# A gate's lower weight halves by accumulating transfers, and a planner's transfer figures refitted

## The chip, the cores and the metric

The kernel runs on one core of one Trainium2 chip. The metric is the device time of one execution in microseconds, and the median of several executions is what is compared.

## What is computed

The reference is a backbone of two layers over 256 latent and 256 context tokens of width 1024, all in float32. Each layer is a half-step SwiGLU feed-forward block (FFN1), a token mixer, and a second half-step block (FFN2), each with a shift, a scale and a gate that come from a conditioning vector ("adaLN"); the last layer carries the latent tokens alone from the mixer on. Cut to what matters here:

```python
mod = (silu_c @ w_ada[l] + b_ada[l])[:, None, :]
sh1, sc1, g1, sh2, sc2, g2, sh3, sc3, g3 = jnp.split(mod, N_MOD, axis=-1)
x = x + 0.5 * g1 * swiglu(modulate(rmsnorm(x), sh1, sc1), ffn1_w1[l], ffn1_w3[l], ffn1_w2[l])
...
o_lat, o_ctx = token_mixer(...)
x = x + g2 * o_lat
x = x + 0.5 * g3 * swiglu(modulate(rmsnorm(x), sh3, sc3), ffn2_w1[l], ffn2_w3[l], ffn2_w2[l])
```

The mixer has one combined input projection. One part of it is the retention branch's output gate, `ret_g` (1024 columns): the branch's result is `silu(g_raw) * n @ w_ret_out`, where `n` is the normalised retention. The change concerns the weights of this part.

## The kernel before

**Precision by three products.** Every float32 product with weights is made of three matmuls in a reduced 32-bit type: upper half of the weights by upper half of the activations, lower half by upper half, upper half by lower half (`mm3`). The weights come as chunks of 128 x 1024 float32 (512 KB) that SP loads into one of four `raw` buffers. `split_w` (L564) makes the two halves of a chunk: ScalarE (ACT in the profile) casts `raw` into one of four `wh` buffers, and VectorE (DVE) subtracts that from `raw` into one of four `wl` buffers:

```python
hi, lo = plan.new("wh", n, F32R), plan.new("wl", n, F32R)
act.copy(out=hi, in_=raw)
dve.tensor_tensor(out=lo, in0=raw, in1=hi, op=ALU.subtract)
```

**FFN steps.** A step of an FFN block multiplies the normalised tokens by one chunk of the first and one of the third weight matrix. ACT takes one PSUM result `m` through SiLU into `t`; DVE multiplies `t` by the other (`t<-t,m`), ACT or DVE casts the product to its upper half (`CAST t<-t`), and DVE subtracts for the lower half (`t<-t,t`). This is called the product chain below. Later steps multiply both halves by the second weight matrix, and DVE adds the result to the residual (`x<-m,mod,x`).

**adaLN beside it.** The conditioning products are done on DVE, not on PE: each chunk of `w_ada` (512 KB, also through the `raw` buffers) is multiplied by the broadcast vector `crow` and summed along its row by one SCALAR_TENSOR_TENSOR, `junk<-raw,crow`, once or twice for a chunk (latent and context vector). `ada_fill` (L781) puts these between the steps of the FFN blocks and `ada_flush` (L786) puts the rest at their end.

**The mixer's gate stage.** After the other projections, a loop at L1433 goes over eight chunks of the gate's weights. `g_step(i)` (L1117) makes 24 matmuls from a chunk (512 columns in layer 0, 256 in layer 1), a Tanh on ACT and one DVE operation. Around it stand the retention's steps for heads in pairs: state, scores, masks, output with a normalisation (statistics on DVE, a power on GpSimd, here POOL: `s<-s,mhalf`), and splits of queries and keys. POOL also multiplies masks (128x384, 128x128) and subtracts for some lower halves (`64x512` in layer 0, `64x256` in layer 1).

**What sets the order.** Nothing is issued while the program is built: every instruction becomes a `Node` with a cost, and `order()` (L249) runs a list scheduler over all nodes with a model of each engine, of buffers (slots of each kind) and of transfers; the order that it finds for each engine is then emitted (`emit`, L358; all of it has line L368). In the model an SP transfer occupies SP for 475 ns, starts at least 1100 ns after its issue, behind the one before, and runs at 400 bytes a ns. At the program's start, PE is given `N_KEEP` = 5 fills (matmuls on a tile of ones, `a<-ones`, in a range of low priority, L1524) beside 20 first ones.

Of the kernel before, what the change touches and what calls it, by code (L numbers as in the profile page):

```python
# [14 lines left out]
AF = mybir.ActivationFunctionType  # L15
# [27 lines left out]
N_PE_ADA = 5  # L43
N_KEEP = 5
URGENT = 1000
# [114 lines left out]
class Node:  # L160


    __slots__ = ("calls", "engine", "cost", "table", "port", "prio", "index", "waits", "after", "bufs", "new", "ready", "start", "end")

    def __init__(self, engine, prio, index):
        self.engine, self.prio, self.index = engine, prio, index
        self.calls, self.cost, self.table, self.port = [], 0.0, None, False
        self.waits, self.after, self.bufs, self.new = set(), [], {}, []
        self.ready, self.start, self.end = 0.0, None, None


class Plan:
# [8 lines left out]

    COLD = 7000.0

    def __init__(self, tc):
# [64 lines left out]
    def order(self):  # L249
# [16 lines left out]
        stuck = {k: [] for k in self.kinds}  # L266
        dma, table, port = 0.0, None, 0.0
        for n in nodes:
# [19 lines left out]
        while len(done) < len(nodes):  # L288
# [36 lines left out]
            if e == "SP":  # L325
                clock[e] = now + 475.0
                n.end = dma = max(now + 1100.0, dma) + n.cost
            else:
                if n.table not in (None, table):
                    now, table = now + self.TABLE, n.table  # L330
                if n.port:

                    now = max(now, port)
                    port = now + n.cost
                slow = 2.0 if e == "PE" and now < self.COLD else 1.0
                n.end = clock[e] = now + slow * n.cost
# [35 lines left out]
class Engine:  # L372
# [5 lines left out]
    def __getattr__(self, method):  # L378
        call = getattr(self.real, method)

        def record(*args, **kwargs):
            views = [v for v in list(args) + list(kwargs.values()) if isinstance(v, View)]
            out = [v for k in ("out", "accum_out") if isinstance(v := kwargs.get(k), View)]
            if "out" not in kwargs and args and isinstance(args[0], View):
                out.append(args[0])
            reads = [v for v in views if not any(v is o for o in out)]

            table = {AF.Silu: 0, AF.Exp: 1, AF.Tanh: 1}.get(args[2]) if method == "activation" else None
            return self.plan.add(self.name, call, args, kwargs, out, reads, self.cost(method, out, reads, kwargs), table,
                                 self.port(method, out, reads, kwargs))  # L390

        return record

    def port(self, method, out, reads, kwargs):

        if self.name == "POOL":
            return method != "memset"
        if self.name != "DVE" or any(v.buf.kind in ("m", "a") for v in out + reads):
# [4 lines left out]
    def cost(self, method, out, reads, kwargs):  # L403
# [5 lines left out]
        if self.name == "SP":  # L409
            return big.shape[0] * n * 4 / 400.0  # L410
        if self.name == "PE":
# [10 lines left out]
        if self.name == "ACT":  # L422
            return 0.834 * n + (50.0 if psum else 93.0) + 91.0 * pointers + (96.0 if "accum_out" in kwargs else 0.0)
        if self.name == "POOL":
            if kwargs.get("op") == ALU.pow:
                return 300.0 + 165.0 * n
# [10 lines left out]
def kernel(  # L437
# [121 lines left out]
    def step(fn, *chunks):  # L559
        steps.append((chunks, fn))  # L560

    def split_w(raw, n, kind):
# [8 lines left out]
        else:  # L571
            hi, lo = plan.new("wh", n, F32R), plan.new("wl", n, F32R)
            act.copy(out=hi, in_=raw)
            dve.tensor_tensor(out=lo, in0=raw, in1=hi, op=ALU.subtract)
        return Pair(hi, lo)
# [377 lines left out]
    def mixer(l, nrm_in, nrm_out, full):  # L953
# [485 lines left out]
        for i in range(8):  # L1439
            if i % 2 == 0:  # L1440
                step(ret_state(i // 2))
                step(ret_scores(i // 2))
                if i >= 2:
                    step(ret_out(i // 2 - 1))
            step(g_step(i), W("g", i))
            if i % 2 == 0:
# [290 lines left out]
```

## Time and profile before

| | us |
|---|---|
| median of three executions | 2145.7 |
| lowest, highest | 2140.36, 2147.9 |
| the profiled execution, its own time | 2144.34 |
| its span in the profile | 2142.6 |
| PE busy | 2112.4 (99%) |
| DVE busy | 1402.9 (65%) |
| ACT busy | 745.1 (35%) |
| POOL busy | 150.6 (7%) |
| mean granted clock of PE | 0.991 |

All rows come from the one profiled execution. A busy PE is one on which matmuls follow each other; at half the clock the same matmuls take longer and PE is just as busy, so the number of matmuls in a stretch says more than the busy share. The page counts one matmul of the program as one or, where it is not in the reduced type, as two records. The chain that ended last is followed back from the last instruction through whatever released each step. The full page has 40 slices of the span, which are too coarse for stalls of a few microseconds: those are read from the timeline of PE, in which each row ends with the idle time ahead of it.

### The profile page before, as it was taken

The page shows a single profiled execution, that of the slowest core. Times are in us where ns is not written, and L with a number is a line of the kernel's source. Part 1 is how long each engine was busy: PE and PEld are TensorE (multiplying, and loading weights), DVE is VectorE, ACT ScalarE, POOL GpSimd, SP SyncE. Part 2 cuts the span into 40 slices and gives each one's busy share as a digit, 9 for nine tenths or more (in the row PEclk, how much of TensorE's full clock was granted, in tenths as well). Part 3 has the DMA queues.
Part 4 walks back from the last instruction along what each step waited for, and adds up shares of the span by engine and source line. Part 5 has one row for each costly group of instructions (what it writes and reads, how often), then busy time and mean ns, then how long its engine had stood idle before and what let it go on. Part 6 is the DMA issues. An engine that isn't in the chain of part 4 may idle for free.

```text
span 2142.6 us, 29830 instructions
## 1 busy us (share of the span) xinstructions
PE 2112.4 (99%) x11630; PEld 1800.7 (84%) x11630; DVE 1402.9 (65%) x2599; ACT 745.1 (35%) x1225; POOL 150.6 (7%) x172
## 2 busy tenths in 40 slices
PE   9999999999999999999999999999999999999998
PEld 6888788987788888988878898888889879999998
DVE  6898785668679435888755473433337967766665
ACT  4222122476433223422212242221225744344433
POOL 0000000211132000100000010000002112100000
PEclk8999999999999999999999999999999999999999
DMA  8476564221121433466665432333233312474663
GB/s 315 148 219 190 181 189 141 91 84 60 60 70 60 128 112 104 138 199 212 189 187 175 139 119 70 109 97 97 90 98 95 116 60 88 149 264 142 205 187 109
DMA packets 87070, 293.76 MB, mean 137 GB/s; under 512 B 9617, under 2 KB 12817, under 8 KB 86929
## 3 DMA queue, kind: packets, MB, share of 16 engines
q1 hardware_dynamic: 86930, 291.87, 43.6%
q8 instruction: 91, 1.49, 0.3%
q14 instruction: 49, 0.40, 0.1%
HBM read 290.78 MB, written 1.05 MB: 136 GB/s over the span
## 4 chain that ended last, share of the span: by engine, by line
PE 71%; DVE 11%; issue 8%; DMA 7%; POOL 1%; ACT 0%; SPq 0%; POOLq 0%; DVEq 0%; ACTq 0%
PE m L368 66%; DMA raw<-in_w_ada_dram 5%; PE a L368 5%; DVE junk L368 5%; DVE t L368 3%; DVE wl L368 2%; DMA t<-in_w_ada_dram 1%; DVE s L368 1%; DVE u L368 1%; POOL s L368 0%; DMA wh<-in_w_ada_dram 0%; POOL t L368 0%; DVE x L368 0%; ACT t L368 0%; DMA raw<-in_w3a_dram 0%
## 5 line engine op out<-in xcount | busy, mean ns | idle before, releaser
L368 PE MATMUL m<-t,wh 128*128 128x512 f32 (+1 forms) x6248 | 1646.8, 351 | 12.2 <-DVE t L368 11.8
L368 PEld LDWEIGHTS m<-t,wh 128*128 128x128 f32 x6248 | 1092.8, 189 | 180.7 <-DVE t L368 14.9
L368 PE MATMUL m<-t,wl 128*128 128x512 f32 (+1 forms) x3124 | 1086.0, 349 | 0.0
L368 ACT CAST wh<-raw 128x1024 fp32r<-128x1024 f32 (+1 forms) x398 | 409.2, 1029 | 959.3 <-PE m L368 824.6
L368 PEld LDWEIGHTS m<-t,wl 128*128 128x128 f32 x3124 | 589.3, 189 | 82.4
L368 DVE TENSOR_TENSOR wl<-raw,wh 128x1024 fp32r<-128x1024 f32 (+1 forms) x398 | 476.5, 1198 | 259.6 <-ACT wh L368 258.6
L368 DVE SCALAR_TENSOR_TENSOR junk<-raw,crow 128x1024 f32<-128x1024 f32 x220 | 268.8, 1222 | 109.9 <-DMA raw<-in_w_ada_dram 106.6
L368 DVE SCALAR_TENSOR_TENSOR x<-m,mod,x 128x256 f32<-128x256 f32 x192 | 86.3, 479 | 124.4 <-PE m L368 124.1
L368 ACT ACTIVATE t<-m 128x512 f32<-128x512 f32 (+1 forms) x155 | 79.3, 513 | 248.1 <-PE m L368 244.0
L368 DVE TENSOR_TENSOR t<-t,t 128x512 fp32r<-128x512 f32 (+7 forms) x252 | 145.4, 585 | 5.0 <-ACT t L368 2.4
L368 DVE TENSOR_TENSOR t<-t,m 128x512 f32<-128x512 f32 (+1 forms) x91 | 54.3, 597 | 109.2 <-PE m L368 103.7
L368 POOL TENSOR_TENSOR s<-s,mhalf 128x2 f32<-128x2 f32 (+1 forms) x31 | 35.5, 1149 | 1163.4 <-DVE s L368 1163.2
L368 PE MATMUL m<-wh,t 128*128 128x512 f32 x288 | 92.1, 399 | 0.0
L368 PE MATMUL a<-t,t 128*64 128x256 f32 (+3 forms) x512 | 87.2, 351 | 4.8 <-DVE t L368 2.8
L368 PEld LDWEIGHTS a<-t,t 128*128 128x128 f32 (+1 forms) x512 | 66.0, 175 | 22.3 <-ACT t L368 4.9
L368 PE MATMUL m<-t,t 128*128 128x256 f32 (+1 forms) x480 | 76.0, 310 | 0.3 <-DVE t L368 0.3
L368 PEld LDWEIGHTS m<-t,t 128*128 128x128 f32 x480 | 65.2, 191 | 5.5 <-issue 1.2
L368 PEld LDWEIGHTS m<-wh,t 128*128 128x128 f32 x288 | 53.2, 188 | 12.6 <-issue 1.2
L368 ACT CAST t<-t 128x512 fp32r<-128x512 f32 (+4 forms) x112 | 55.9, 526 | 11.5 <-DVE t L368 8.9
L368 PE MATMUL m<-wl,t 128*128 128x512 f32 x144 | 56.9, 395 | 0.0
L368 ACT ACTIVATE t<-u,mod 128x256 fp32r<-128x256 f32 x88 | 39.7, 500 | 28.8 <-DVE u L368 28.8
L368 POOL MEMSET t<- 32x512 f32 x32 | 16.1, 528 | 473.7 <-DVE junk L368 257.3
(105 smaller groups left out, 1045.7 us busy)
## 6 DMA issues: line engine op xcount, KB each, us to landing
raw<-in_w_ada_dram SPq DMA_DIRECT2D x122, 512.0 KB, 4.2
raw<-in_w_m_dram SPq DMA_DIRECT2D x76, 512.0 KB, 3.5
raw<-in_w1b_dram SPq DMA_DIRECT2D x44, 512.0 KB, 3.9
raw<-in_w3b_dram SPq DMA_DIRECT2D x44, 512.0 KB, 3.8
raw<-in_w1a_dram SPq DMA_DIRECT2D x41, 512.0 KB, 3.6
raw<-in_w3a_dram SPq DMA_DIRECT2D x41, 512.0 KB, 3.6
raw<-in_w2a_dram SPq DMA_DIRECT2D x32, 512.0 KB, 3.5
raw<-in_w2b_dram SPq DMA_DIRECT2D x32, 512.0 KB, 3.6
```

Of the source, the lines that this page charges most:

```text
L368: call(*[resolve(v) for v in args], **{k: resolve(v) for k, v in kwargs.items()})
```

## The change

Three things are changed.

1. In both layers the gate's chunks get the kind "d". For these, ACT writes `-raw` into the lower buffer (a second ACT operation on the chunk), rounded as the type of that buffer demands, and a transfer issued by POOL adds `raw` to it: what is left is `raw` less its rounded value. There are 16 such chunks, so 16 DVE subtractions go, 16 ACT operations and 16 transfers inside SBUF come. The chunk's `raw` buffer is now held until the transfer has landed.
2. The planner's figures for transfers are others: the first may start at 2000 ns, an issue takes 560 ns, a transfer starts at least 2000 ns after it and runs at 380 bytes a ns. A transfer on POOL is billed 870 ns of POOL, 2913 ns of the transfers' time and 1800 ns until its end is seen.
3. `N_KEEP` is 20.

```diff
-N_KEEP = 5
+N_KEEP = 20
...
+    FIRST, ISSUE, LATENCY, RATE = 2000.0, 560.0, 2000.0, 380.0
...
-        dma, table, port = 0.0, None, 0.0
+        dma, table, port = self.FIRST, None, 0.0
...
             if e == "SP":
-                clock[e] = now + 475.0
-                n.end = dma = max(now + 1100.0, dma) + n.cost
+                clock[e] = now + self.ISSUE
+                n.end = dma = max(now + self.LATENCY, dma) + n.cost
+            elif n.moved:
+                clock[e] = now + n.cost
+                dma = max(now + self.LATENCY, dma) + n.moved
+                n.end = dma + 1800.0
...
+            if self.name == "POOL" and method == "dma_start":
+                node.moved += 1.5 * out[0].shape[0] * math.prod(out[0].shape[1:]) * 4 / 270.0
...
-            return method != "memset"
+            return method not in ("memset", "dma_start")
...
-            return big.shape[0] * n * 4 / 400.0
+            return big.shape[0] * n * 4 / Plan.RATE
...
+            if method == "dma_start":
+                return 870.0
...
             act.copy(out=hi, in_=raw)
-            dve.tensor_tensor(out=lo, in0=raw, in1=hi, op=ALU.subtract)
+            if kind == "d":
+                act.activation(lo, raw, AF.Copy, scale=-1.0)
+                pool.dma_start(out=lo, in_=raw, accum_op=ALU.add)
+            else:
+                dve.tensor_tensor(out=lo, in0=raw, in1=hi, op=ALU.subtract)
...
-            step(g_step(i), W("g", i))
+            step(g_step(i), W("g", i, "d"))
```

Since the planner's figures enter every decision of `order()`, operations move on DVE, ACT, PE and POOL far from the gate stage too. SP issues the same transfers in the same order, and PE does the same matmuls but for 15 more fills. Of the fills, before the change two stood ahead of the first matmul of the first FFN step and three a little later, each ahead of one accumulation group; now seven stand ahead of the first matmul and thirteen (eleven of them in a row) at the later place. At the start PE also broadcasts `crow` by eight small matmuls: before, three of them stood among the matmuls of the first norms; now all eight stand ahead of these.

**VectorE near the end of FFN1 in layer 0**, before the change. `junk` is an adaLN sum, `t2_1853<-t2_1853,m1_1849` the product of the last FFN step, the CAST and `t11_1921` its two halves, `mod` a finished modulation, `wl` a chunk's lower half:

```order
L368 SCALAR_TENSOR_TENSOR junk_66,s14_1610<-raw0_1797,crow_65 128x1024
L368 TENSOR_TENSOR wl0_1865<-raw1_1770,wh0_1855 128x1024
L368 TENSOR_SCALAR mod0_5_98<-mod0_5_98 128x8
L368 TENSOR_TENSOR mod0_5_98<-s14_1610,sm_64 128x8
L368 TENSOR_SCALAR mod0_5_98<-mod0_5_98 128x8
L368 SCALAR_TENSOR_TENSOR junk_66,s15_1889<-raw0_1867,crow_65 128x1024
L368 TENSOR_TENSOR t2_1853<-t2_1853,m1_1849 128x512
L368 TENSOR_TENSOR wl1_1904<-raw2_1832,wh1_1895 128x1024
L368 CAST t48_1909<-t2_1853 128x512
L368 SCALAR_TENSOR_TENSOR junk_66,s16_1916<-raw0_1867,crow_65 128x1024
L368 TENSOR_TENSOR t11_1921<-t2_1853,t48_1909 128x512
```

The same place after the change:

```order
L375 SCALAR_TENSOR_TENSOR junk_66,s14_1653<-raw3_1818,crow_65 128x1024
L375 TENSOR_TENSOR wl0_1883<-raw0_1796,wh0_1870 128x1024
L375 TENSOR_SCALAR mod0_5_98<-mod0_5_98 128x8
L375 TENSOR_TENSOR mod0_5_98<-s14_1653,sm_64 128x8
L375 TENSOR_SCALAR mod0_5_98<-mod0_5_98 128x8
L375 TENSOR_TENSOR t0_1868<-t0_1868,m2_1864 128x512
L375 CAST t3_1914<-t0_1868 128x512
L375 TENSOR_TENSOR wl1_1916<-raw2_1845,wh1_1908 128x1024
L375 TENSOR_TENSOR t10_1924<-t0_1868,t3_1914 128x512
L375 SCALAR_TENSOR_TENSOR junk_66,s15_1931<-raw3_1885,crow_65 128x1024
L375 SCALAR_TENSOR_TENSOR junk_66,s16_1939<-raw3_1885,crow_65 128x1024
```

The product, the cast and the lower half now stand ahead of the two sums on the chunks that came last; before, one sum stood ahead of the product and one between the cast and the lower half. The `wl` now stands behind the cast.

**VectorE in the gate stage of layer 1**, before the change, where the query of a head is split (`t20`, CAST) and a gate's result `t42` is multiplied:

```order
L368 TENSOR_TENSOR t20_14992<-t9_14266,t20_14992 64x256
L368 CAST t14_15001<-t22_13728 64x256
L368 TENSOR_TENSOR wl3_15064<-raw1_14874,wh3_15044 128x1024
L368 SCALAR_TENSOR_TENSOR t42_15054<-t42_15054,m1_14982 128x256
L368 BN_STATS s20_15088<-a3_15042 128x6
L368 BN_STATS s31_15090<-a3_15042 128x6
L368 BN_AGGR s36_15096<-s20_15088 128x2
```

The same place after the change:

```order
L375 TENSOR_TENSOR t41_15045<-t8_14289,t41_15045 64x256
L375 CAST t0_15050<-t10_13751 64x256
L375 TENSOR_TENSOR t33_15060<-t10_13751,t0_15050 64x256
L375 TENSOR_TENSOR t26_15095<-t10_13751,t43_15022 64x256
L375 SCALAR_TENSOR_TENSOR t37_15090<-t37_15090,m0_15006 128x256
L375 BN_STATS s20_15112<-a0_15069 128x6
L375 BN_STATS s31_15116<-a0_15069 128x6
L375 BN_AGGR s36_15122<-s20_15112 128x2
```

The lower weight half between the cast and the gate's product has gone.

**GpSimd in the gate stage of layer 1**, before the change: lower halves (64x256), masks (128x384 and 128x128) and the power of a head pair's normalisation (`s34`):

```order
L368 TENSOR_TENSOR t26_15012<-t22_13728,t14_15001 64x256
L368 TENSOR_TENSOR t21_14961<-t21_14961,t1_15024 128x384
L368 TENSOR_TENSOR t18_15029<-t18_15029,t45_15037 128x384
L368 TENSOR_TENSOR t21_14961<-t21_14961,ident_77 128x128
L368 TENSOR_TENSOR t47_15067<-t22_13728,t35_15035 64x256
L368 TENSOR_TENSOR t18_15029<-t18_15029,ident_77 128x128
L368 TENSOR_TENSOR s34_15129<-s35_15123,mhalf_85 128x4
```

And after it, where DMA is an accumulating transfer into a lower weight half:

```order
L375 TENSOR_TENSOR t12_14846<-t43_13715,t33_14833 64x256
L375 DMA wl3_14889<-raw1_14615 128x1024
L375 DMA wl1_14918<-raw2_14706 128x1024
L375 DMA wl2_14949<-raw3_14796 128x1024
L375 DMA wl0_14998<-raw0_14853 128x1024
L375 TENSOR_TENSOR t20_14985<-t20_14985,t26_15027 128x384
L375 TENSOR_TENSOR t33_15060<-t10_13751,t0_15050 64x256
L375 TENSOR_TENSOR t20_14985<-t20_14985,ident_77 128x128
L375 TENSOR_TENSOR t14_15034<-t14_15034,t29_15041 128x384
L375 TENSOR_TENSOR t36_15088<-t10_13751,t32_15067 64x256
L375 DMA wl3_15082<-raw1_14931 128x1024
L375 TENSOR_TENSOR t14_15034<-t14_15034,ident_77 128x128
```

Four transfers stand in a row ahead of the masks, one stands between them, and the first power comes behind all of these.

## Rows read from the trace of the kernel before

**Rows 1.** the page: busy time of the engines, and the chain that ended last

```profile
PE 2112.4 (99%) x11630; PEld 1800.7 (84%) x11630; DVE 1402.9 (65%) x2599; ACT 745.1 (35%) x1225; POOL 150.6 (7%) x172
...
PE 71%; DVE 11%; issue 8%; DMA 7%; POOL 1%; ACT 0%; SPq 0%; POOLq 0%; DVEq 0%; ACTq 0%
```

**Rows 2.** timeline of PE: start, duration, operation, [idle before <-releaser]

```profile
233.25 0.79 PE L368 MATMUL m<-t,wh 128*128 128x512 f32 x1 [4.17 <-DVE t L368]
...
1082.20 0.50 PE L368 MATMUL m<-t,wh 128*128 128x512 f32 x1 [1.28 <-DVE t L368]
...
1083.93 0.73 PE L368 MATMUL m<-t,wh 128*128 128x512 f32 x2 [1.00 <-DVE t L368]
...
1814.48 0.39 PE L368 MATMUL m<-t,wh 128*128 128x256 f32 x1 [1.45 <-DVE t L368]
...
1826.11 0.36 PE L368 MATMUL a<-t,t 128*128 128x256 f32 x1 [1.45 <-ACT t L368]
...
1828.66 1.32 PE L368 MATMUL a<-t,t 128*128 128x256 f32 x4 [1.09 <-DVE t L368]
...
1831.27 0.58 PE L368 MATMUL m<-t,wh 128*128 128x256 f32 x1 [1.29 <-DVE t L368]
```

**Rows 3.** stretches: PE, PEld, DVE, ACT, POOL busy (x), clock, DMA share, GB/s

```profile
200.00:220.00 20.00, 20.00 (x88) 16.13 (x87) 14.06 (x21) 5.19 (x6) 0.00 (x0) 1.00 0.61 184
...
220.00:240.00 20.00, 15.31 (x57) 11.53 (x56) 17.19 (x32) 2.10 (x2) 0.00 (x0) 0.83 0.56 175
...
1080.00:1100.00 20.00, 17.71 (x69) 13.59 (x69) 12.46 (x21) 3.16 (x3) 0.00 (x0) 0.91 0.59 185
...
1800.00:1820.00 20.00, 18.55 (x161) 18.34 (x160) 19.30 (x48) 11.52 (x26) 6.69 (x8) 1.00 0.23 72
...
1820.00:1840.00 20.00, 15.65 (x106) 14.69 (x105) 17.37 (x48) 5.45 (x11) 4.96 (x6) 0.83 0.22 74
...
1840.00:1860.00 20.00, 20.00 (x172) 20.00 (x171) 14.26 (x26) 9.37 (x14) 1.93 (x1) 1.00 0.66 204
...
590.00:700.00 110.00, 109.14 (x623) 94.35 (x622) 94.20 (x230) 39.10 (x62) 31.23 (x26) 1.00 0.21 67
```

**Rows 4.** timeline of DVE before the stall at 229 us

```profile
229.90 1.23 DVE L368 SCALAR_TENSOR_TENSOR junk<-raw,crow 128x1024 f32<-128x1024 f32 x1 [1.98 <-DMA raw<-in_w_ada_dram]
...
231.05 0.68 DVE L368 TENSOR_TENSOR t<-t,m 128x512 f32<-128x512 f32 x1
...
232.78 0.42 DVE L368 CAST t<-t 128x512 fp32r<-128x512 f32 x1
```

**Rows 5.** timeline of DVE before the stall at 1082 us

```profile
1078.82 1.23 DVE L368 SCALAR_TENSOR_TENSOR junk<-raw,crow 128x1024 f32<-128x1024 f32 x1 [3.14 <-DMA raw<-in_w_ada_dram]
```

**Rows 6.** group of DVE from 1780 to 1840 us (busy, mean ns), and one row

```profile
L368 DVE TENSOR_TENSOR wl<-raw,wh 128x1024 fp32r<-128x1024 f32 x9 | 11.0, 1220 | 0.1
...
1829.66 1.23 DVE L368 TENSOR_TENSOR wl<-raw,wh 128x1024 fp32r<-128x1024 f32 x1
```

**Rows 7.** the page's groups and DMA issues: casts, loads of mixer chunks

```profile
L368 ACT CAST wh<-raw 128x1024 fp32r<-128x1024 f32 (+1 forms) x398 | 409.2, 1029 | 959.3 <-PE m L368 824.6
...
raw<-in_w_m_dram SPq DMA_DIRECT2D x76, 512.0 KB, 3.5
```

**Rows 8.** timeline of POOL, and of DVE beside it, in layer 1's gate stage

```profile
1788.85 1.49 POOL L368 TENSOR_TENSOR t<-t,ident 128x128 f32<-128x128 f32 x1 [0.24 <-ACT t L368]
...
1791.23 0.46 POOL L368 TENSOR_TENSOR t<-t,ident 128x128 f32<-128x128 f32 x1
...
1788.80 1.22 DVE L368 TENSOR_TENSOR wl<-raw,wh 128x1024 fp32r<-128x1024 f32 x1
```

**Rows 9.** timeline of PE at the start: a broadcast of crow, and two fills

```profile
22.53 1.22 PE L368 MATMUL m<-crow,ones 1*128 1x256 f32 x2
...
49.16 0.38 PE L368 MATMUL a<-ones 128*128 128x128 f32 x2
...
50.07 0.38 PE L368 MATMUL a<-ones 128*128 128x128 f32 x2
```

More of the change, by code (lines that the diff above doesn't have):

```diff
@@ L160 @@
 class Node:
-    __slots__ = ("calls", "engine", "cost", "table", "port", "prio", "index", "waits", "after", "bufs", "new", "ready", "start", "end")
+    __slots__ = ("calls", "engine", "cost", "table", "port", "moved", "prio", "index", "waits", "after", "bufs", "new", "ready", "start", "end")
     def __init__(self, engine, prio, index):
         self.engine, self.prio, self.index = engine, prio, index
-        self.calls, self.cost, self.table, self.port = [], 0.0, None, False
+        self.calls, self.cost, self.table, self.port, self.moved = [], 0.0, None, False, 0.0
         self.waits, self.after, self.bufs, self.new = set(), [], {}, []
@@ L388, in record @@
             table = {AF.Silu: 0, AF.Exp: 1, AF.Tanh: 1}.get(args[2]) if method == "activation" else None
-            return self.plan.add(self.name, call, args, kwargs, out, reads, self.cost(method, out, reads, kwargs), table,
+            node = self.plan.add(self.name, call, args, kwargs, out, reads, self.cost(method, out, reads, kwargs), table,
                                  self.port(method, out, reads, kwargs))
+            if self.name == "POOL" and method == "dma_start":
+                node.moved += 1.5 * out[0].shape[0] * math.prod(out[0].shape[1:]) * 4 / 270.0
+            return node
         return record
```

## The prediction

> **What bounds the kernel now.** The page comes first: PE is busy for 99% of the span, DVE for 65%, and the chain that ended last runs through PE for 71%, through DVE for 11% and through transfers for 7% [rows 1]. No engine beside PE can be the bound over the whole span, and no matmul is taken away, so the change can win only where PE stands idle or is granted half its clock. The second view is therefore PE's timeline, searched for idle time: there are few stalls, and the large ones wait for DVE, or for ACT behind it [rows 2]. Those that this change can reach lie in three places: near the end of FFN1 in layer 0 (4.17 us before 233.25), near the end of FFN2 in layer 0 (1.28 and 1.00 before 1084), and in the gate stage of layer 1 (four waits of 1.09 to 1.45 between 1813 and 1831). Idle time is not the whole loss. The third view counts matmuls in stretches of 20 us [rows 3]: a full stretch of 512 columns holds 88, the one with the first stall 57 at a granted clock of 0.83, the one at 1080 holds 69 at 0.91. With 256 columns 172 are full, and 1820 to 1840 holds 106 at 0.83. The granted clock falls to the lower of its two levels after the long or repeated stalls; with the single 1.45 us at 1814 it stays at 1.00 from 1800 to 1820. So the reader should see short holes whose price is up to twice their length.
>
> **FFN1 of layer 0, the stall at 229.** Missing matmuls: 31, at 20/88 = 0.227 us, so 7.0 us. DVE's rows say why [rows 4]. It falls idle at 229.90 - 1.98 = 227.92, waiting for an adaLN chunk, while the product of the last FFN step stands behind that sum and starts only at 231.05, and the cast, behind a `wl`, at 232.78; another sum follows ahead of the lower half. In the new order no sum stands between the modulation and the product, and none between cast and lower half. From 227.92: product 0.68 and cast 0.42 at the rows' durations, so the upper half is there by 229.02, just before PE runs dry at 233.25 - 4.17 = 229.08. A `wl` (1.22) now follows, and the lower half (0.68, like the product) by 230.9. PE has two matmuls of 0.23 to do meanwhile and wants it at 229.5: up to 1.4 us of idle time is left, about 1.0 as such rows overlap a little, less than the 1.45 that left the clock alone. Term: -7.0 + 1.0 = **-6.0**. Its ends are -7.0 and 0 (the sums were only moved, and may be late elsewhere).
>
> **FFN2 of layer 0, the stall at 1082.** 19 matmuls are missing, 4.3 us. Here one sum still stands ahead of the product in the new order, like the one that waited 3.14 us for its chunk [rows 5], but another, that stood ahead of the cast, is moved behind the lower half. That makes both halves about 1.2 us earlier: the 1.28 goes, most of the 1.00 stays, and the clock should hold. 4.3 - 1.0 would be 3.3; since the chunk may come later I take **-2.5**, ends -4.3 and 0.
>
> **Layer 1's gate stage.** Missing matmuls: 66 at 20/172 = 0.116, so 7.7 us, and the 1.45 before it: 9.1 us to be had. DVE is busy 19.3 of 20 us from 1800 [rows 3], and from 1780 to 1840 it makes nine lower weight halves of 1.22 us [rows 6]; the stage has eight of the kind that goes. Two of PE's waits, 1.45 at 1814 and 1.29 at 1831, end on a DVE operation behind such a `wl` (the one at 1829.66 for the second): 1.2 of each goes, 2.4. The 1.45 and 1.09 between them, 2.5, stand in a DVE queue of which 11.0 us in 60 are `wl`; I take half, 1.3, because the power and the masks that they also need now wait behind transfers on POOL. That is 3.7 of 5.3 us idle. Of the other 3.8 of the loss, mostly the clock, I take a third: **-5.0**. Ends -9.1 and 0; the other sign is a rival.
>
> **What the lower half now costs.** In the same stage ACT gets eight operations more, 1.03 each as its cast [rows 7]; with 5 to 12 of 20 us busy [rows 3] they lie beside PE's work. An accumulating transfer does not occur in the trace. From below: a load of the same size takes 3.5 us from issue to landing [rows 7]. From above: it reads two buffers and writes one, so two such loads, 7.0, and a POOL operation as slow as one beside a `wl`, 1.49 [rows 8]: 8.5. With the ACT operation a lower half is ready 4.5 to 9.5 us behind its upper half, instead of 1.2. I take 6, as it has the load's rows and bytes to write. The chunks follow each other every 60/9 = 6.7 us with four buffers of each kind, so with up to 27 us of lead; even 9.5 is hidden. The chunk's `raw` buffer is held some 5 us longer in such a cycle of 27, which is hidden too, and the transfers have time for it: their share is 0.22 to 0.23 there [rows 3]. In layer 0 PE is busy for 109.14 of the 110 us from 590 to 700, so 0.86 is to be gained at most, and a gate step is longer, since a matmul has twice the columns: I take **0**, ends -0.9 and 0.
>
> **The start.** Of 15 more fills, ten stand in the dense part, where one fill and a group of three matmuls follow each other every 50.07 - 49.16 = 0.91 us [rows 9], of which the three take 0.68: 0.23 each, 2.3. Five stand in the part at half the clock, at twice that: 2.3. Against that, three broadcasts leave this part, where one takes 1.22 [rows 9], half of which is then saved: 1.8. Net +2.8 on PE. Whether PE or DVE sets the end of this part no row shows. With PE the bound it is +2.8, and +4.6 if the broadcasts save nothing; with DVE the bound the fills cost nothing, and an earlier `crow` gives 1.8. I take a value near the middle, **+1.0**, ends -1.8 and +4.6.
>
> **Sum.** -6.0 - 2.5 - 5.0 + 0 + 1.0 = -12.5. The profiled execution took 2144.3, which gives 2131.8; it stands 1.4 (0.06%) below the median of 2145.7, and the forecast is **2132**. A difference under 0.3%, 6.4 us, can't be told from none by a measurement of this kernel: faster means below 2139.3, slower above 2152.1.
>
> **Rival 1: the adaLN waits come back elsewhere.** There are as many sums and loads as before, and a sum that is moved behind the product holds its `raw` buffer longer. For it: the waits of 1.98 and 3.14 us are waits for transfers [rows 4, 5]. Against: PE needs no sum until the gate of the next residual. Then -6.0 and -2.5 fall away, and -5.0 + 1.0 are left: 2144.3 - 4.0, about **2140**, no change.
>
> **Rival 2, slower: POOL's queue.** Four transfers in a row stand ahead of two masks and a lower half that PE's steps need, a fifth and more ahead of the power. Each waits for ACT's write, which waits for PE to release a `wl`. If one is held, everything behind it on POOL is late. It decides when POOL's item comes later by more than DVE's shorter queue makes up, 2.4 us. Price: two more microseconds for each of the four head pairs of both layers, 16, and 2 us of clock at half of them, as at 1080 (4.3 missing, 2.3 idle): 24. With the FFN terms and the start, -7.5: **2161**. Against: POOL is busy in only 5 to 7 of 20 us [rows 3].
>
> **Rival 3, slower: issues stretched by DVE.** On POOL the same 128x128 product took 0.46 us, and 1.49 where DVE was in a `wl` from 1788.80 [rows 8]. If each issue is stretched so, 1.03 more, and lies on PE's path, 16 x 1.03 = 16.5 are added and -5.0 is lost: 2144.3 - 7.5 + 16.5, about **2153**. Against: the `wl` that stretched it is among those that go. The Trainium skill, page "SBUF — State Buffer", section "SBUF: two separate sides", warns of this: GpSimd itself writes the descriptors of a DMA from its queue, and cannot while DVE holds the port pair that they share, as a float32 copy makes it do. By that rule the transfers start late and the time is this rival's; no row here shows descriptors being written, only the stretched product agrees.
>
> **How the numbers follow.** The forecast gets 0.66: three holes, each with an operation that visibly leaves or moves, and two of them nearly suffice. Rival 1 gets 0.20, rival 2 0.10, rival 3 0.04. Faster 0.66, same 0.20, slower 0.14. The range begins at 2122, where nearly every term is at its better end (all of them would be 2144.3 - 7.0 - 4.3 - 9.1 - 0.9 - 1.8 = 2121), and ends at 2150, which takes in rival 1 with the start at +4.6 (2144) and some 6 us of late halves. Left out are rivals 2 and 3 and a little below, under 0.2.
>
> **What would show it.** Right: 80 or more matmuls in the 20 us around the end of FFN1, clock 1.00 there; the gate stage of layer 1 with under 3 us idle and no `wl` on DVE. Wrong: waits of PE ended by `wl`, or by a DVE operation behind POOL; a wait of about 4 us for an adaLN sum at another place; the row that stood at 49.16 coming more than 5 us late.

## The result, and the profile after

| | us |
|---|---|
| the changed kernel, median of four executions (lowest, highest) | 2123.36 (2119.92, 2127.44) |
| the kernel before, median of four | 2146.16 |
| ratio, 95% interval | 0.9899, 0.9873 to 0.9925 |
| profiled execution of the changed kernel, its own time, span | 2123.66, 2121.9 |

The change makes the kernel 1.0% faster, by 20.7 us from span to span. The forecast was 2132 with a range from 2122 to 2150; the time lies in it, close to its lower end. The gain has the forecast sign and is some 1.7 times the forecast size.

The page of the changed kernel first (busy time; the chain that ended last; the group of the adaLN sums, with idle time ahead of it):

```profile
PE 2103.9 (99%) x11660; PEld 1799.1 (85%) x11660; DVE 1389.0 (65%) x2583; ACT 760.2 (36%) x1241; POOL 159.1 (7%) x188
...
PE 90%; issue 6%; DVE 3%; POOL 1%; ACT 0%; POOLq 0%; DVEq 0%; ACTq 0%
...
L375 DVE SCALAR_TENSOR_TENSOR junk<-raw,crow 128x1024 f32<-128x1024 f32 x220 | 268.6, 1221 | 48.6 <-DMA raw<-in_w_ada_dram 46.2
```

The same group before:

```profile
L368 DVE SCALAR_TENSOR_TENSOR junk<-raw,crow 128x1024 f32<-128x1024 f32 x220 | 268.8, 1222 | 109.9 <-DMA raw<-in_w_ada_dram 106.6
```

Beside [rows 1], the chain that ended last has lost steps through DVE (11% to 3%) and its steps through transfers (7% to none): it is nearly all PE. PE's busy time fell by 8.5 us although 30 fill records came: matmuls ran at a higher clock (mean granted clock 0.996, before 0.991). DVE waits 46.2 us for adaLN chunks in all, where it waited 106.6 before.

PE's timeline after the change has four waits of 1 us or more between the first fills and the last norm:

```profile
611.71 1.55 PE L375 MATMUL a<-t,t 128*128 128x256 f32 x9 [1.06 <-DVE t L375]
...
885.55 0.39 PE L375 MATMUL m<-t,wh 128*128 128x256 f32 x1 [1.08 <-DVE t L375]
...
1807.99 0.93 PE L375 MATMUL a<-t,t 128*128 128x256 f32 x4 [1.09 <-DVE t L375]
...
1810.60 0.58 PE L375 MATMUL m<-t,wh 128*128 128x256 f32 x1 [1.68 <-DVE t L375]
```

Of [rows 2], the 4.17, the 1.28 and the 1.00 have gone altogether, and of the layer 1 waits the first two; 1.09 is still there, and the last has grown from 1.29 to 1.68. The wait at 611.71, in the gate stage of layer 0, is new. The 1.08 at 885.55, at the beginning of layer 0's FFN2, was 2.10 before:

```profile
898.06 0.38 PE L368 MATMUL m<-t,wh 128*128 128x256 f32 x1 [2.10 <-DVE t L368]
```

Stretches, with the columns of [rows 3]:

```profile
15.00:20.00 5.00, 5.00 (x38) 3.80 (x35) 2.66 (x8) 2.44 (x7) 0.00 (x0) 0.74 1.06 391
...
205.00:225.00 20.00, 20.00 (x88) 16.16 (x87) 16.70 (x30) 4.69 (x5) 0.00 (x0) 1.00 0.62 193
...
1060.00:1080.00 20.00, 20.00 (x88) 16.22 (x87) 12.43 (x19) 3.16 (x3) 0.00 (x0) 1.00 0.69 212
...
1780.00:1800.00 20.00, 20.00 (x174) 19.94 (x174) 19.25 (x54) 13.65 (x29) 8.38 (x10) 1.00 0.75 190
...
1800.00:1820.00 20.00, 17.17 (x118) 16.47 (x117) 17.31 (x47) 6.39 (x12) 4.98 (x6) 0.83 0.21 70
```

The two places in FFN blocks (205 to 225, 1060 to 1080) now hold the full 88 matmuls at full clock, where 57 and 69 stood. "End of FFN1" and "end of FFN2" in the texts ahead are loose names for them: each block adds to the residual in three groups of steps, and both stalls stand at the end of the second group (in the trace before, FFN1 of layer 0 goes on to 411 us, FFN2 to 1260). The second half of layer 1's gate stage holds 118, against 106 before, and the clock still falls to 0.83 there. At the start, 15 to 20 us, the clock is 0.74.

**Where the time came from, place by place.** DVE's operations of the form `t<-t,m` (an FFN product or a gate's product) are 139 in every trace, in the same sequence, so the n-th of one trace can be set against the n-th of another. The table gives their start less that in the trace of the kernel before, in us, at nine of them. The first row is the time in the trace before; `after` is the changed kernel, the other rows are the experiments below.

```
          first  FFN1   layer 0 gate  FFN2    layer 1 gate  gates  last
          FFN    l.0,   stage         l.0     stage         l.1    FFN
          prod.  late   in     out    end     in     out    end    l.1
before    65.3  297.8  625.7  715.5  1213.8  1789.9 1830.8 1914.8 2103.7
after     -4.5  -12.8  -12.8  -11.8  -17.0   -17.1  -20.7  -20.0  -21.4
e12       -3.6  -11.9  -11.9  -10.9  -16.2   -16.3  -19.8  -19.4  -20.5
e1        -3.2  -11.1  -11.1  -10.1  -15.1   -16.3  -19.8  -20.3  -21.0
e2         2.2    4.2    4.2    4.2    2.1     1.7    1.7    1.0    0.9
e3        -2.5  -10.7  -10.8  -10.7  -15.5   -15.6  -15.7  -15.4  -15.4
e4         0.0   -7.8   -7.9   -7.8  -12.6   -13.9  -13.9  -13.9  -14.5
e5        -0.3   -1.3   -1.2   -0.2    3.3     3.0   -0.5   -2.8   -3.8
e6        -3.6  -11.9  -11.9  -11.9  -16.6   -16.9  -20.5  -21.3  -21.7
e7        -1.8  -10.1  -10.1   -9.1  -14.4   -14.5  -14.5  -14.3  -15.1
e8        -0.7   -8.4   -8.6   -7.7  -12.4   -12.4  -15.9  -16.4  -17.1
e9        -5.6  -11.7  -11.9  -11.8  -16.7   -18.1  -21.6  -20.7  -21.4
e10       -3.3  -11.6  -11.7  -11.7  -16.4   -16.7  -22.5  -20.7  -21.4
e11       -2.0  -10.3  -10.4  -10.3  -15.1   -15.4  -21.0  -23.1  -23.6
```

Read along the row `after`: 4.5 us are won at the start, 8.3 in FFN1, 1.0 is lost in layer 0's gate stage, 5.2 are won up to the end of FFN2 of layer 0, 3.6 in layer 1's gate stage, 0.7 given back behind it, and 1.4 won in the rest. The border between the first two is not sharp, as the first product stands in a full DVE queue (busy for 5.00 of 5 us from 60 to 65). ACT's SiLU of the step just ahead of the stall (218.0 us before) comes 5.4 earlier than before and the next one, behind it, 12.8 earlier: by these, the start gives 5.4 and the stall 7.3. The stall gives 7.3 to 7.4 in each of the eleven kernels with the new figures.

### The profile page after: what moved, and what is told of

It is laid out like the page before. It is cut to its first block, busy times and chain, and to the rows that moved or that the text cites. A ratio compares the mean times of both kernels' runs of the same rounds, so it can differ in the third digit from the quotient of the medians.

```text
span 2121.9 us, 29939 instructions
## 1 busy us (share of the span) xinstructions
PE 2103.9 (99%) x11660; PEld 1799.1 (85%) x11660; DVE 1389.0 (65%) x2583; ACT 760.2 (36%) x1241; POOL 159.1 (7%) x188
## 3 DMA queue, kind: packets, MB, share of 16 engines
HBM read 290.78 MB, written 1.05 MB: 138 GB/s over the span
## 4 chain that ended last, share of the span: by engine, by line
PE 90%; issue 6%; DVE 3%; POOL 1%; ACT 0%; POOLq 0%; DVEq 0%; ACTq 0%
PE m L375 83%; PE a L375 7%; DVE t L375 2%; DVE u L375 1%; DVE s L375 1%; POOL s L375 0%; DVE wl L375 0%; POOL t L375 0%; ACT t L375 0%; ACT wh L375 0%; ACT wl L375 0%; POOLq L1749 0%; DVE x L375 0%; ACT u L375 0%; POOL ident masks.py:197 0%
## 5 line engine op out<-in xcount | busy, mean ns | idle before, releaser
L375 DVE TENSOR_TENSOR wl<-raw,wh 128x1024 fp32r<-128x1024 f32 (+1 forms) x382 | 457.9, 1200 | 245.8 <-ACT wh L375 244.9
L375 DVE SCALAR_TENSOR_TENSOR junk<-raw,crow 128x1024 f32<-128x1024 f32 x220 | 268.6, 1221 | 48.6 <-DMA raw<-in_w_ada_dram 46.2
L375 ACT ACTIVATE t<-u,mod 128x256 fp32r<-128x256 f32 x88 | 39.9, 500 | 25.2 <-DVE u L375 22.7
```

Source lines behind the costliest of these rows:

```text
L375: call(*[resolve(v) for v in args], **{k: resolve(v) for k, v in kwargs.items()})
```

## The experiments

The theories were these. **T**, the prediction's: the new figures clear the FFN stalls, the accumulating transfers give some 5 us in layer 1 and nothing in layer 0, and the late fills cost PE 0.23 us each. Against it, after the traces had been compared: **F**, the fills make the shorter start; **O**, the new order alone makes it; **A**, the transfers give 3 to 4 in layer 1 and cost 1 in layer 0.

### The three parts apart

e1, e2, e3 and e4 ran on one chip, against 2145.2 for the kernel before; e5 and e8 on one chip with two runs further below, against 2146.2.

e1, five fills:

```diff
-N_KEEP = 20
+N_KEEP = 5
```

> The changed kernel with N_KEEP 5 instead of 20; the new figures put all five fills ahead of the first FFN matmul (1, 2 and 2), where 20 put seven there and thirteen later. Theory of the prediction (late fills cost PE 0.23 us each, ten of them 2.3): 2 us faster than the changed kernel, about 2121. Rival F (the number of fills is what made the start 6 us shorter): the start is lost, 2129. Rival O (the order of the broadcasts and a few early fills made it): 2123 to 2125, and the first residual stands within 1 us of the changed kernel's 122.1.

Measured: 2124.94, ratio 0.9913 (0.9899 to 0.9926). The gain of 2 us did not come. The first product is at -3.2, within the spread that seven kernels with 20 fills show (below). The time is rival O's, and no cost of the late fills is seen here. Its second condition is not met: the first residual stands at 124.2, 2.1 behind the changed kernel's 122.1.

e2, the kernel before with 20 fills:

```diff
-N_KEEP = 5
+N_KEEP = 20
```

> The kernel before with N_KEEP 20 and nothing else: under the old figures all the extra fills go behind the first groups of the first FFN step, none ahead of its first matmul. Theory of the prediction: 15 late fills at 0.23 us, 3.5 us slower than before (2149.6). Rival F (more fills shorten the start): 2140. Rival O: the clock stays at half until 30 us as before, and the late fills are hidden or not: 2146 to 2149, no gain.

Measured: 2147.59, ratio 1.0013 (1.0001 to 1.0025): 2.4 us slower. By place the start loses 2.2 and FFN1 2.0 more, since its stall grew from 4.17 to 6.01 us:

```profile
237.72 0.80 PE L368 MATMUL m<-t,wh 128*128 128x512 f32 x1 [6.01 <-DVE t L368]
```

Rival F, that more fills as such shorten the start, is out: under the old figures none of the extra fills stands ahead of the first FFN matmul. The loss at the start is what a cost of the fifteen more late fills would look like, at two thirds of T's 3.5, though one trace does not settle a start that closely (below).

e3, no accumulating transfers:

```diff
-            step(g_step(i), W("g", i, "d"))
+            step(g_step(i), W("g", i))
```

> The changed kernel with the gate's lower halves from DVE again (kind w in both layers); new figures and 20 fills stay. Theory of the prediction (the accumulating transfers give 5 us in layer 1 and nothing in layer 0): 2128. Rival A (they give 3 in layer 1 and cost 1 in layer 0, as the comparison of the two traces by place suggests): 2125 to 2126. Rival P (DVE's relief is hidden, the layer 1 gain is the planner's order): 2122 to 2124.

Measured: 2128.36, ratio 0.9925 (0.9913 to 0.9938), the number of T. By place, though, layer 0's stage shows no loss (-10.8 in, -10.7 out), and layer 1's no gain: -15.6 in, -15.7 behind it. The four waits of before are all there again (1.44, 1.42, 1.09 and 1.68); the first two on PE's timeline:

```profile
1798.80 0.38 PE L375 MATMUL m<-t,wh 128*128 128x256 f32 x1 [1.44 <-DVE t L375]
...
1810.43 0.36 PE L375 MATMUL a<-t,t 128*128 128x256 f32 x1 [1.42 <-ACT t L375]
```

So the layer 1 gain belongs to the transfers, not to the new figures, and rival P is out.

e4, the new figures alone (e3's edit and five fills):

> Only the new planner figures: kind w, N_KEEP 5. Theory of the prediction: the two FFN stalls go, 8.5 us, and the start gains 1.8 from the broadcasts: 2136. Rival O (the order by the new figures makes the start, both ends of the FFN blocks and the beginning of FFN2): 18 us less than before, 2127. Rival F (fills make the start): 2133.

Measured: 2127.96, ratio 0.9925 (0.9913 to 0.9937), some 17 of the 22.8 us. By place 7.8 come in FFN1, 4.8 in FFN2 of layer 0, 1.3 more before layer 1's gate stage, and at the first product, in this trace, nothing. T's number of 2136 was 8 too high, O's was right but not by its reason: the start gave nothing here. e4's order at the start is e1's, yet the first products are 3.2 apart. The traced execution of e4 is the slowest of its six (2129.80), that of e1 the fastest (2123.80). The medians of e3 and e4, 20 fills and 5 without the transfers, are alike, 2128.36 and 2127.96.

e5, the transfers alone, under the old figures for SP's loads and with five fills:

```diff
-    FIRST, ISSUE, LATENCY, RATE = 2000.0, 560.0, 2000.0, 380.0
+    FIRST, ISSUE, LATENCY, RATE = 0.0, 475.0, 1100.0, 400.0
...
-N_KEEP = 20
+N_KEEP = 5
```

> Only the accumulating transfers: the planner's figures for SP are the old ones (0, 475, 1100, 400), N_KEEP 5; POOL's transfers are billed as in the change. Theory of the prediction (5 us in layer 1, nothing in layer 0): 2140 against a before of 2145. Rival A (3 to 4 us in layer 1, a cost of 1 in layer 0): 2142. Rival C (the transfers need the new figures, or the start changes with them): 2146 or more.

Measured: 2142.59, ratio 0.9982 (0.9970 to 0.9994): 3.6 faster. By place the stage of layer 0 costs 1.0 and that of layer 1 gives 3.5, as with the new figures. FFN1's stall is still there:

```profile
231.38 0.79 PE L375 MATMUL m<-t,wh 128*128 128x512 f32 x1 [2.58 <-DVE t L375]
```

FFN2 of layer 0 loses 3.5 in this order. The figures, not the transfers, clear the FFN stalls.

e8, no fills:

```diff
-N_KEEP = 20
+N_KEEP = 0
```

> The changed kernel with N_KEEP 0: the broadcasts still stand ahead of the norms, no fill in the first 60 us beside the first 20. Theory of the prediction (fills only cost): 4 us faster than the changed kernel, 2119. Rival O (the order of the broadcasts made the start): 2123. Rival F (the fills between the norms' matmuls bring the clock back early): half the clock until about 30 us as before, the first residual 4 to 6 us later than the changed kernel's 122.1, 2128.

Measured: 2128.68, ratio 0.9921 (0.9908 to 0.9934), F's number; T's 2119 is far off. The first product is at -0.7, the first residual at 126.5, 4.4 behind the changed kernel's. From 15 to 20 us, the kernel before and this one (columns as above):

```profile
15.00:20.00 5.00, 5.00 (x16) 3.26 (x12) 1.39 (x5) 2.54 (x6) 0.00 (x0) 0.50 1.05 381
```

```profile
15.00:20.00 5.00, 5.00 (x21) 3.01 (x19) 1.08 (x2) 2.55 (x6) 0.00 (x0) 0.50 1.05 380
```

Both are granted half the clock through this stretch; the changed kernel 0.74, with 38 matmul records in place of 16 and 21. F's other condition, half the clock until about 30 us, fails: without a fill the clock is back at about 23.7, in the kernel before at 30. e8 first, then the kernel before:

```profile
22.50:25.00 2.50, 2.50 (x13) 1.81 (x12) 1.83 (x6) 0.59 (x2) 0.00 (x0) 0.77 1.04 389
```

```profile
30.00:32.50 2.50, 2.50 (x20) 1.84 (x22) 1.05 (x4) 0.28 (x1) 0.00 (x0) 0.98 1.00 399
```

So in this trace the new order alone has the clock back some 6 us sooner, and by the first product wins only 0.7 with it. With no fills PE then waits near 60 us:

```profile
61.08 0.74 PE L375 MATMUL m<-t,t 128*128 128x512 f32 x2 [1.16 <-ACT t L375]
...
62.46 2.56 PE L375 MATMUL m<-t,t 128*128 128x512 f32 x10 [0.65 <-DVE t L375]
```

So under the new figures some fills are better than none: e8's five times are 2126.69 to 2129.83, the changed kernel's eight (after and e12) 2119.92 to 2127.44. By place it is 1 to 4 us, as the seven kernels with 20 fills and the new figures (after, e12, e3, e6, e7, e10, e11) have their first product between -1.8 and -4.5. What 20 give over 5 is not settled: e1 and e4 have -3.2 and 0.0, and the times of e3 and e4 show nothing. The spread is between programs whose order is the same there (for after and e12 it is the same program), so one trace does not settle a start to better than some 3 us. Among the seven it goes with the moment at which the clock is back. From 17.5 to 20 us the granted clock is 0.97, 0.89, 0.85 and 0.62 in after, e12, e6 and e10, whose first products are at -4.5, -3.6, -3.6 and -3.3; in e3, e11 and e7 it is 0.50 there and 0.65, 0.51 and 0.50 in the 2.5 us behind, with -2.5, -2.0 and -1.8. It is not all of it: e4 has its clock back at about 22.7, like e7, and its first product 1.8 later.

### The two layers apart

e6 and e7, on the same chip as e5 and e8:

```diff
-            step(g_step(i), W("g", i, "d"))
+            step(g_step(i), W("g", i, "d" if l else "w"))
```

> The changed kernel with the accumulating transfers in layer 1 alone. Theory of the prediction (layer 0 nothing): as the changed kernel, 2123.4. Rival A (the transfers cost 1 us in layer 0's gate stage): about 1 us faster than the changed kernel by place, the offset at the end of layer 0's gate stage stays where it was at its start, and layer 1 still gains 3 or more.

Measured: 2122.02, ratio 0.9892 (0.9878 to 0.9906). By place: no loss in layer 0, 3.6 won in layer 1.

e7 has `"w" if l else "d"`:

> The changed kernel with the accumulating transfers in layer 0 alone. Theory of the prediction: layer 1's 5 us are lost, 2128.4. Rival A: layer 1's 3.4 are lost and the cost of 1 in layer 0 stays: 2127 to 2129, 1 us behind the kernel without them if the start is alike.

Measured: 2128.01, ratio 0.9919 (0.9906 to 0.9931). By place: 1.0 lost in layer 0, nothing in layer 1.

The table decides for rival A without an exception: all six kernels with the transfers in layer 0 (after, e12, e1, e5, e7, e8) lose 0.9 to 1.0 between 625.7 and 715.5, and none of the other seven loses over 0.1. All kernels with them in layer 1 win 3.5 to 5.8 between 1789.9 and 1830.8, and the other four (e2, e3, e4, e7) nothing.

What layer 0 pays for is seen in the changed kernel. DVE's timeline:

```profile
595.98 3.06 DVE L375 TENSOR_TENSOR t<-t,t 64x512 fp32r<-64x512 f32 x1
...
598.96 1.49 DVE L375 CAST t<-t 64x512 fp32r<-64x512 f32 x1
...
610.28 1.37 DVE L375 TENSOR_SCALAR t<-a,s,s 128x128 f32<-128x128 f32 x4 [0.91 <-POOL s L375]
```

and POOL's:

```profile
592.30 0.87 POOL L375 DMA_DIRECT2D wl<-raw  x1 [4.69 <-ACT wl L375]
...
594.67 1.06 POOL L375 TENSOR_TENSOR t<-t,t 128x384 f32<-128x384 f32 x1 [1.50 <-DVE t L375]
...
595.69 1.40 POOL L375 TENSOR_TENSOR t<-t,t 64x512 fp32r<-64x512 f32 x1
...
597.47 1.01 POOL L375 TENSOR_TENSOR t<-t,t 128x384 f32<-128x384 f32 x1
...
598.56 1.61 POOL L375 TENSOR_TENSOR t<-t,t 64x512 fp32r<-64x512 f32 x1
...
609.00 1.25 POOL L375 TENSOR_TENSOR s<-s,mhalf 128x4 f32<-128x4 f32 x1 [2.60 <-DVE s L375]
```

POOL sat 4.69 us in front of a transfer, for ACT's write, but that did not hold up what follows: behind the transfer it waited 1.50 more, for DVE. Then it ran two masks, two 64x512 subtractions and, at 597.05, a 128x128 mask, from 594.67 to 600.16 with no gap above 0.1 us. DVE's 64x512 subtraction fell into that time and took 3.06 us, the cast behind it 1.49. In e3 POOL has its first 64x512 subtraction ahead of the masks, and gaps between them:

```profile
596.65 1.28 POOL L375 TENSOR_TENSOR t<-t,t 64x512 fp32r<-64x512 f32 x1 [40.23 <-ACT t L375]
...
598.63 1.05 POOL L375 TENSOR_TENSOR t<-t,t 128x384 f32<-128x384 f32 x1 [0.69 <-DVE t L375]
...
599.98 1.50 POOL L375 TENSOR_TENSOR t<-t,t 128x384 f32<-128x384 f32 x1 [0.29 <-DVE t L375]
```

The same operations on DVE in e3:

```profile
599.93 0.69 DVE L375 TENSOR_TENSOR t<-t,t 64x512 fp32r<-64x512 f32 x1
...
600.54 1.23 DVE L375 CAST t<-t 64x512 fp32r<-64x512 f32 x1
...
610.50 1.37 DVE L375 TENSOR_SCALAR t<-a,s,s 128x128 f32<-128x128 f32 x4 [0.20 <-POOL s L375]
```

The subtraction takes 0.69 there. It takes 3.05 to 3.06 in all six kernels with the transfers in layer 0 and 0.68 to 0.69 in the eight without. From its start to the end of the second pair's statistics DVE needs 12.9 us here (595.98 to 608.92) and 9.2 in e3 (599.93 to 609.15); the two stretched operations are 2.6 of the difference, and the rest is the order of the others. By these rows, what the transfers took off DVE here (in e3 a `wl` stands at 593.19 and one at 602.00) came back as stretched operations; the statistics and the power came later against PE (the power waits for DVE's statistics, and DVE's idle time for the power grows from 0.20 to 0.91), and PE waits the 1.06 of the row at 611.71. That the new order of POOL stretches DVE's operations is read from these rows; no run puts POOL's order back alone.

### Late fills, and a better version

e9, the transfers in layer 1 alone, `N_KEEP = 8`: the seven early fills stay and one late fill. e9 to e12 ran on one chip, against 2146.2.

> Accumulating transfers in layer 1 alone, N_KEEP 8: the seven early fills stay where they are, of the thirteen late ones one is left. Theory of the prediction (late fills cost 0.23 each on PE): 2.8 us faster than with 20, 2119. Rival H (PE stands ahead of DVE there, and late fills only fill its wait): same time as with 20, 2122, and PE's waits of 0.6 each near 60 us are back.

Measured: 2122.60, ratio 0.9888 (0.9872 to 0.9905), as rival H has it. The first product comes early, at -5.6, and then PE waits:

```profile
56.14 0.73 PE L375 MATMUL m<-t,t 128*128 128x512 f32 x2 [1.01 <-ACT t L375]
...
57.53 4.14 PE L375 MATMUL m<-t,t 128*128 128x512 f32 x10 [0.65 <-DVE t L375]
```

and from 55 to 65 us its clock is 0.83:

```profile
55.00:65.00 10.00, 8.34 (x29) 6.26 (x29) 10.00 (x17) 2.70 (x5) 0.00 (x0) 0.83 0.60 201
```

where the changed kernel has 1.00 and 45 matmuls. Late in FFN1 the lead is -11.7, within 0.2 of e6. The twelve late fills stand in a wait that PE would have anyway, and keep its clock.

e10 and e11 ask why PE's last wait in layer 1's gate stage grew to 1.68. On DVE of the changed kernel:

```profile
1808.99 1.22 DVE L375 TENSOR_TENSOR wl<-raw,wh 128x1024 fp32r<-128x1024 f32 x1
...
1810.13 0.41 DVE L375 SCALAR_TENSOR_TENSOR t<-t,m 128x256 f32<-128x256 f32 x1
```

The lower half at 1808.99 is of the next stage's second chunk (the latent branch's gate, `gm`; the first chunk's stands at 1796.73), not one of those that the change moved, and the gate's product that PE waits for stands behind it. e10 gives all eight `gm` chunks of layer 1 the transfers too, e11 the first two:

```diff
-                step(gate("gm", m), W("gm", m))
+                step(gate("gm", m), W("gm", m, "d" if l and m < 2 else "w"))
```

> Accumulating transfers in layer 1 for the output gate and for all eight chunks of the gate of the latent branch (gm), N_KEEP 20. Theory W (a lower half of the next gate's first chunk on DVE stands ahead of the product that PE waits 1.68 us for at the end of the gate stage): that wait shrinks to 0.5 and the clock drop behind it goes, 2 to 4 us faster than with the output gate alone, 2118 to 2120. Rival Q (POOL's queue or ACT takes over as the late one): 2122 to 2125.

> As the run before, but only the first two of the eight gm chunks. Theory W: the same gain, 2118 to 2120, since only the first stands in the gate stage. Rival Q: 2122 or more.

Measured: e10 2121.97, ratio 0.9887 (0.9871 to 0.9903); e11 2120.09, ratio 0.9878 (0.9861 to 0.9896). On PE's timeline of e11 the two waits are 0.30 and 0.55:

```profile
1808.76 0.93 PE L375 MATMUL a<-t,t 128*128 128x256 f32 x4 [0.30 <-DVE t L375]
...
1810.24 0.38 PE L375 MATMUL m<-t,wh 128*128 128x256 f32 x1 [0.55 <-DVE t L375]
```

and the stretch is full to 161 matmuls at a clock of 1.00:

```profile
1800.00:1820.00 20.00, 19.15 (x161) 18.62 (x160) 18.82 (x54) 7.97 (x16) 6.54 (x8) 1.00 0.50 148
```

By place both win 5.6 to 5.8 in the stage instead of 3.5; e10 gives 1.8 back in the gates, where PE waits for one of its transfers, while e11 wins 2.1 more:

```profile
1838.33 0.38 PE L375 MATMUL m<-t,wl 128*128 128x256 f32 x1 [1.95 <-DMA wl<-raw]
```

Theory W holds for the wait and the clock; its number for e10 was 2 too low. Its reason in e11, that only the first `gm` chunk stands in the gate stage, is not exact: both lower halves of e11 stood there on DVE.

e12, the changed kernel again, beside them:

> The changed kernel once more, as it is, beside the three runs above on one chip. By the first measurement 2123.4; by the comparison by place, 1 us behind a kernel with the transfers in layer 1 alone. If its first residual's place varies with the moment at which the clock returns, it stands between 121.5 and 124.5 us.

Measured: 2123.92, ratio 0.9895 (0.9879 to 0.9911). Its first product is 0.9 later than in the first trace, with the clock back later, its first residual at 123.0, and the rest is the same to 0.3 by place. e11's highest time is 2121.5 and this one's lowest 2121.38, though the two intervals overlap; by place, behind FFN1, e11 is 4.7 ahead of e12 ((23.6 - 10.3) against (20.5 - 11.9)). e11 has the lowest median of this study; its interval overlaps those of e6, e9 and e10 too.

## Why the prediction was right, and where its sizes were off

**The sign and the main mechanism** were right: the two places in FFN blocks of layer 0 hold 88 matmuls, the clock is 1.00, and e4 and e5 show that the new figures do it, through the order. The criterion for the gate stage was half met: 2.83 of 40 us idle from 1780 to 1820, but lower halves of the next stage on DVE.

**FFN1, -6.0 forecast, -8.3 measured** by the table, 7.3 of it at the stall: the term's better end, -7.0. The step that was mis-sized is the idle time that was to be left, "about 1.0 as such rows overlap a little". It took DVE's place in time, free at 227.92, from the old trace. DVE after the change, from its last modulation on:

```profile
216.23 0.17 DVE L375 TENSOR_SCALAR mod<-mod 128x8 f32<-128x8 f32 x1
...
218.13 0.69 DVE L375 TENSOR_TENSOR t<-t,m 128x512 f32<-128x512 f32 x1 [1.73 <-PE m L375]
...
218.85 0.43 DVE L375 CAST t<-t 128x512 fp32r<-128x512 f32 x1
...
220.35 0.69 DVE L375 TENSOR_TENSOR t<-t,t 128x512 fp32r<-128x512 f32 x1
...
220.96 1.22 DVE L375 SCALAR_TENSOR_TENSOR junk<-raw,crow 128x1024 f32<-128x1024 f32 x1
```

DVE is free 1.73 us before PE delivers the product's operand, the sum on the last chunks follows at 220.96, and PE never runs dry. DVE had caught up: its waits for adaLN chunks fell by 60 us over the program, and from 17.5 to 4.2 us in 100 to 240 us. I had moved the operations and left the waits where they were.

**FFN2 of layer 0, -2.5 forecast, -5.2 measured.** The same error: all of the 4.3 us went, though one sum still stands ahead of the product and still waits for its chunk, 2.07 us in place of 3.14 [rows 5]:

```profile
1062.88 1.23 DVE L375 SCALAR_TENSOR_TENSOR junk<-raw,crow 128x1024 f32<-128x1024 f32 x1 [2.07 <-DMA raw<-in_w_ada_dram]
```

The wait at the block's beginning, which had no term, gave 1.0 (2.10 to 1.08).

**The start, +1.0 forecast, -4.5 measured** (-1.8 to -4.5 in the kernels with the same start). This step was wrong, and its range, -1.8 to +4.6, too: the fills were costed by their own duration on PE, and the moment at which the clock comes back had no term. In the seven kernels with 20 fills and the new figures it came back 7 to 12 us sooner (between 17.6 and 22.7 us, at 30 before). Some 6 of these come without any fill (e8, 23.7), where the first product gained only 0.7, so the return alone does not account for the gain. The late fills lay in a wait under the new figures (e9), as the end with DVE as the bound had it; under the old ones the kernel with them is 2.4 slower (e2). That it takes more than the broadcasts follows from e8 against the others; how the gain divides between order, fills and clock stays open, since e4, with five fills, shows a late return and e1, with the same start, an early one.

**Layer 1's gate stage, -5.0 forecast, -3.6 measured, with 0.7 given back.** The step that failed is that two of PE's waits "end on a DVE operation behind such a `wl`": this holds for the first, and the one at 1829.66 [rows 6] is the next stage's. Of the nine halves of [rows 6] five are of the gate, and four are later ones that the change leaves. e11 shows what it would have been with the next stage's first two away too.

**Layer 0's gate stage, 0 forecast, +1.0 measured.** It has the sign of Rival 2 and a twelfth of its price for the layer, but not its way: the power that PE's wait hangs on waited for DVE, not behind a transfer, and DVE's operations were stretched beside POOL's. The sum left it out because PE had 0.86 to gain there; that it could lose was not in the term's ends.

**What a lower half costs** was sized well. ACT's and POOL's part in layer 1 (min/median/max ns):

```profile
L375 ACT ACTIVATE wl<-raw x8: 1051/1053/1057, 1749.2 to 1787.5; 128x1024 fp32r<-128x1024 f32 x8
...
L375 POOL DMA_DIRECT2D wl<-raw x8: 860/890/972, 1750.6 to 1790.4; - x8
```

and from issue to landing, all sixteen (median us):

```profile
wl<-raw POOLq DMA_DIRECT2D x16, 512.0 KB, 5.8
```

ACT 1.05 and 5.8 make 6.9 behind the upper half; 6 was taken, 4.5 to 9.5 the bounds. It is hidden in layer 1's gate stage: no wait of PE there ends on a transfer. In e10, with more of them behind the stage, one does, 1.95 us.

**Rival 3** did not happen. Two of POOL's issues in layer 1 fall in the 20 us in which DVE was busy for 19.25:

```profile
1781.91 0.86 POOL L375 DMA_DIRECT2D wl<-raw  x1 [3.07 <-ACT u L375]
...
1790.35 0.90 POOL L375 DMA_DIRECT2D wl<-raw  x1
```

They took no longer than the other six (0.86 to 0.97), which fall in stretches of 20 us with DVE busy for 3.35 and 14.38. The warning of the Trainium skill, "SBUF — State Buffer", section "SBUF: two separate sides", on transfers from GpSimd's queue is not borne out by these rows, as far as an issue's duration shows it. They are no hard test of it: the warning names a float32 copy on DVE, beside these two issues DVE ran none, and when the descriptors were written, no row shows. What the same section says of the lock between DVE and GpSimd instructions, that one waits for the whole of the other, agrees with the subtraction of 3.06 us beside POOL's masks and subtractions.

**Rival 1** did not happen either: no wait for an adaLN sum came back on PE.

In sum, of -21.4 by place the forecast had -12.5: by the columns of the table it missed 5.5 at the start, 2.3 in FFN1, 2.7 in FFN2 and 1.4 in the rest, and had 3.1 too much in the two gate stages. By the same columns the start, FFN1 and FFN2 passed their better ends by 2.7, 1.3 and 0.9, and the two gate stages fell short of theirs by 8.1: that the total lies in the range is in part luck.

## What to carry to other kernels

When a static order is changed, don't keep the other engine's waits at their old times: if a wait for a buffer or a load shrinks, everything behind it comes sooner, and a stall that was to shrink may vanish. Before an operation is taken off a busy engine, read which operation stands ahead of the one that PE waits for: here it was the next stage's, and moving two chunks more won another 2 us in the stage by place, while moving all eight gave it back. When transfers go onto GpSimd's queue, look at how its other work is ordered anew: here five of its operations without a gap between them stood beside a VectorE operation that took 3.06 us in place of 0.69.

## What the runs showed of the hardware

- An accumulating transfer of 512 KB inside SBUF took 5.8 us from issue to landing (median of 16), loads of the same size 3.5 to 4.2 (medians by weight matrix).
- A 64x512 subtraction on DVE took 3.06 us beside two masks and two 64x512 subtractions on POOL that left no gap above 0.1 us, and 0.69 where POOL's operations had gaps of 0.3 to 0.7.
- In seven traces with the same order at the start PE's clock was back at different moments, from 17.6 to about 22.7 us, and their first FFN product varied with it by 2.7 us. With no fills the clock was back at 23.7, with the old order at 30.
